# Gate, up and ff1 with tokens stationary, and all moving weights read as two halves of a chunk in turn

## The chip, the cores and the metric

The kernel runs on one core of one Trainium2 chip. The metric is the device time of one execution in microseconds (us), smaller is better. The core's engines are TensorE (PE in the profile, its weight loads PEld), VectorE (DVE), ScalarE (ACT), GpSimd (POOL) and SyncE (SP), which issues nearly all the transfers.

## The reference

Two transformer blocks of width 2048 run one after the other on one sequence of 256 tokens. Cut to what matters here:

```python
def conv_ffn(x, w_gate, w_up, conv_w, conv_b, w_down):        # first block; D_FF = 5632
    hg = x @ w_gate
    hg = causal_conv3_per_channel(hg, conv_w) + conv_b
    return (gelu(hg) * (x @ w_up)) @ w_down

# first block:  h += mix(rmsnorm(h) @ w_in) @ w_out;  h += conv_ffn(rmsnorm(h), ...)
#               h += sigmoid(rmsnorm(h) @ w_ple_gate) * (p @ w_ple_proj)
# second block: mod = silu(c) @ w_mod + b_mod  ->  sh1, sc1, g1, sh2, sc2, g2
#               x += g1 * (attention(h @ w_in_2 ...) @ w_out_2)
#               h = rmsnorm(x) * (1 + sc2) + sh2
#               u = relu(h @ w_ff1)                            # 8192 columns
#               x += g2 * ((u * u) @ w_ff2)
```

All inputs are float32. In total about 510 MB of weights are read once.

## The kernel before

Every dense product is computed in three matmuls of the type float32r. Each operand is split into a high part (a copy rounded to float32r) and a low part (the rest), and high x high, high x low and low x high are accumulated in PSUM.

Weights come in blocks. A block is 256 rows of K by one chunk of 512 output columns (448 or 384 in two chunks), 512 KB, laid out by the host (`_pack`, line 152) so that one transfer fills a tile of 128 partitions x 1024. `prep` (line 273) issues that transfer on SP, has ACT write the high part `whi` (line 281) and DVE the low part `wlo` (line 282). It does so at high priority; there are four buffers of `raw` and three of each part. Some last or first blocks of a stage are kept in tiles of their own (`hold`, names such as `whiaaaaa`). The chunk of K rows that belongs to one matmul is `w[:, j*cw:(j+1)*cw]`, j = 0, 1.

Two forms of product use these blocks:

- `linear` (line 297): 128 tokens are the stationary operand, the weights of one j are the moving operand with `cw` columns (512), and PSUM gets tokens x output columns. A block is 2 token tiles x 2 j x 3 = 12 matmuls (lines 318 to 320). It serves w_in, w_out, w_down, the ple products, w_in2, w_out2, ff2, and the first chunk of ff1.
- `linear_t` (line 346): 128 columns of the weights are the stationary operand and 256 tokens are the moving one, so the result is already transposed (output columns on partitions, tokens along the free dimension), as the convolution over tokens and the next product need it. A block is 4 x 2 x 3 = 24 matmuls of 256 columns (lines 360 to 362). It serves gate and up (11 chunks each) and ff1's chunks 1 to 15. For it, `prep` shifts the weights by 16 elements inside a tile that is 64 elements longer.

Where `linear` is used and a transposed result is wanted, `xt_chunk` (line 385) waits a tick, lets PE transpose four 128x128 pieces into an `aux` bank of PSUM (line 382) and splits the result into high and low parts.

The program is written as a stream of blocks. After each block, `tick` (line 250) moves on the generators that were handed to `spawn`: a generator that yields n goes on n blocks later. `tick` also emits, at a rate `mod_rate` per block, halves of the `w_mod` product (`mod_half`, line 910: a transfer of 512 KB into one of two `wmod` tiles and one multiplication with sum on DVE, line 920). 192 halves are needed, 160 of them before the ple gate; the last 32 run at one per block in ff1. The order of the instructions on each engine is set by a scheduler from priorities and dependencies.

`conv_ffn` (line 963) goes through groups of four chunks (the last has three): gate, then up for each chunk, and the `down` product of a group after the first chunk of the next one. In `conv` (line 981), DVE multiplies the PSUM result by `rb`, the row of 1/rms per token (line 984), ACT applies the first tap and the bias, DVE adds two more taps; after the gelu, DVE multiplies by `rb` again (line 996), for the up product, which `up` (line 1001) takes from PSUM as it is. `mlp2` (line 1402) has the same order with ff1 and ff2 in four groups of four chunks. Its `g2` row comes from the sums of `w_mod`: `mod_row` (line 935) adds up the columns on DVE, transposes them on PE two ticks later (line 940), and writes and reads back a row through DRAM; it is spawned after `ff1(4)`, before the first `ff2`.

Of the kernel before, what the change touches and what calls it, by code (L numbers as in the profile page):

```python
# [9 lines left out]
F32 = mybir.dt.float32  # L10
F32R = mybir.dt.float32r
# [6 lines left out]
P = 128  # L18
# [133 lines left out]
def _pack(w, widths, nk=2):  # L152
    k = w.shape[0]
    out = []
    c0 = 0
    for cw in widths:
        b = w[:, c0:c0 + cw].reshape(k // (nk * P), nk, P, cw).transpose(0, 2, 1, 3)
        out.append(np.ascontiguousarray(b).reshape(-1))
        c0 += cw
    return np.concatenate(out)  # L160


def layout(inputs):
# [25 lines left out]
    a["w_uq"] = _pack(uqc, [CW] * 3, nk=3)  # L189
    ukv = sq("w_ukv_2").reshape(128, 8, 256)  # L190
    a["w_ukv"] = _pack(np.concatenate([ukv[:, :, :128].reshape(128, 1024),
                                       ukv[:, :, 128:].reshape(128, 1024)], axis=1),
                       [2 * CW] * 2, nk=1)
# [11 lines left out]
    return {k: np.ascontiguousarray(v) for k, v in a.items()}  # L205

# [5 lines left out]
class K:  # L212
# [60 lines left out]
    def prep(self, src, ncol, hold=None, shift=False):  # L273
        nc = self.nc
        pool, n, k = (self.HOLD, len(hold), hold) if hold else (self.W, 3, "")
        with self.tc.high_priority():
            raw = self.t(self.W, [P, 1024], "raw", 4)
            self.wdma = nc.sync.dma_start(raw[:, :ncol], src)
            e, s = (0, 0) if hold else (64, 16 * shift)
            hi, lo = (self.t(pool, [P, 1024 + e], w + k, n, F32R)[:, s:s + 1024] for w in ("whi", "wlo"))  # L280
# [16 lines left out]
    def linear(self, xt, name, seq, off, cw, evac, before=None):  # L297
# [9 lines left out]
        def products(c, b, i, w):  # L307
# [6 lines left out]
            for j in range(2):  # L314
                xh, xl = xt(2 * b + j)
                wh = w[0][:, j * cw:(j + 1) * cw]
                wl = w[1][:, j * cw:(j + 1) * cw]
# [27 lines left out]

    def linear_t(self, xt, name, off, evac):


        nc = self.nc
        ps = [self.ps.tile([P, 512], F32, name=self.n("mm"), tag="mm", bufs=4) for _ in range(2)]  # L350
        last = KT // 2 - 1
        for b in range(KT // 2):
            hi, lo = self.prep(self.wblock(name, off + b * 2 * P * CW, 2, CW), 2 * CW, shift=True)
            for m in range(4):
                o = ps[m // 2][:, (m % 2) * T:(m % 2 + 1) * T]
                for j in range(2):
                    xh, xl = xt(2 * b + j)
                    ws = slice(j * CW + m * P, j * CW + (m + 1) * P)
                    first = b == 0 and j == 0 and m % 2 == 0
                    nc.tensor.matmul(o, hi[:, ws], xh, start=first, stop=False, skip_group_check=True)  # L360
                    nc.tensor.matmul(o, hi[:, ws], xl, start=False, stop=False, skip_group_check=True)  # L361
# [1153 lines left out]
```

## Time and profile before

| | us |
|---|---|
| median of 3 runs | 2290.66 |
| lowest and highest | 2286.03, 2298.77 |
| profiled execution, its time | 2293.44 |
| profiled execution, its span (first to last instruction) | 2291.7 |

| engine | busy share of the span | instructions |
|---|---|---|
| PE | 98% | 13714 |
| PEld | 87% | 13714 |
| DVE | 69% | 2329 |
| ACT | 48% | 1560 |

The page of the profile gives busy times per engine, a picture of the span in 40 slices (a digit is tenths busy, for PEclk tenths of the full TensorE clock), and the chain of work that ended last. Views of the trace give single instructions in order of time, groups by line, tables of stretches, and who waited for whom. The durations of matmuls overlap: the next one starts long before the end that is shown, so a rate is read from starts. A name such as `mm<-whi,xt` is the output tile and the operands.

### The profile page before, as it was taken

Reading aid. Unit: us, or ns where it says so; the run is one execution under the profiler, and the core shown is the slowest. Engines: PE = TensorE matmul, PEld = TensorE weight load, DVE = VectorE, ACT = ScalarE, POOL = GpSimd, SP = SyncE. Lnnn points to the kernel's source line nnn. Section 1 sums busy time; section 2 is a strip of 40 time slices with the busy share of each in tenths; the row PEclk is TensorE's granted clock in tenths of the full one; section 3 lists DMA queues with packets and bytes.
Section 4 is the critical chain, followed back from the end, with each engine's and each line's share of the span. In section 5 each row is a group of like instructions: output and inputs, shape, how many; then the busy total and the mean of one; then the engine's idle time right before and its main releaser. Section 6 shows DMA issues by size and latency. Waiting matters only on the chain.

```text
span 2291.7 us, 34932 instructions
## 1 busy us (share of the span) xinstructions
PE 2246.7 (98%) x13714; PEld 1996.9 (87%) x13714; DVE 1573.5 (69%) x2329; ACT 1105.6 (48%) x1560; POOL 25.8 (1%) x35
## 2 busy tenths in 40 slices
PE   9999999999999999999999999999999999999998
PEld 7787887899998999989987788888878998998986
DVE  6777766777876677767777866768766555555555
ACT  6655554454444444434445655655433443443444
POOL 0000000000000000000000000000000000000000
PEclk9999999999999999999999999999999999999999
DMA  8665566677777777777778643566886566656554
GB/s 300 229 211 193 205 230 208 241 254 259 265 264 261 265 252 254 256 258 264 249 255 301 241 161 117 173 194 212 309 290 193 190 187 193 190 187 193 190 188 154
DMA packets 147537, 517.82 MB, mean 226 GB/s; under 512 B 17115, under 2 KB 21292, under 8 KB 146860
## 3 DMA queue, kind: packets, MB, share of 16 engines
q1 hardware_dynamic: 147228, 515.58, 66.3%
q8 instruction: 107, 1.75, 0.3%
q14 instruction: 58, 0.48, 0.1%
q10 hardware_dynamic: 144, 0.01, 0.0%
HBM read 513.38 MB, written 2.14 MB: 225 GB/s over the span
## 4 chain that ended last, share of the span: by engine, by line
PE 80%; DMA 7%; issue 6%; DVE 5%; ACT 1%; POOL 1%; SPq 0%; DVEq 0%; ACTq 0%; POOLq 0%
PE mm L320 14%; PE mm L319 14%; PE mm L318 14%; PE mm L362 11%; PE mm L361 11%; PE mm L360 11%; DMA wmod<-in_w_mod 6%; DVE wlo L282 2%; PE aux L382 1%; DVE wmod L920 1%; PE aux L750 1%; ACT whi L281 1%; DMA raw<-in_w_ff 0%; PE aux L824 0%; PE aux L1273 0%
## 5 line engine op out<-in xcount | busy, mean ns | idle before, releaser
L281 ACT ACTIVATE whi<-raw 128x1024 fp32r<-128x1024 f32 (+1 forms) x746 | 785.9, 1055 | 999.0 <-PE mm L320 539.9
L282 DVE TENSOR_TENSOR wlo<-raw,whi 128x1024 fp32r<-128x1024 f32 (+1 forms) x746 | 905.5, 1216 | 503.6 <-ACT whi L281 501.9
L362 PE MATMUL mm<-xt,wlo 128*128 128x256 f32 x2368 | 662.6, 280 | 5.8 <-DVE wlo L282 5.8
L361 PE MATMUL mm<-xt,whi 128*128 128x256 f32 x2368 | 661.5, 279 | 0.0
L360 PE MATMUL mm<-xt,whi 128*128 128x256 f32 x2368 | 661.5, 279 | 0.0
L361 PEld LDWEIGHTS mm<-xt,whi 128*128 128x128 f32 x2368 | 451.0, 190 | 0.3
L362 PEld LDWEIGHTS mm<-xt,wlo 128*128 128x128 f32 x2368 | 444.6, 188 | 7.4 <-DVE wlo L282 7.2
L360 PEld LDWEIGHTS mm<-xt,whi 128*128 128x128 f32 x2368 | 444.6, 188 | 0.3
L319 PE MATMUL mm<-wlo,hid 128*128 128x512 f32 x848 | 331.4, 391 | 1.0 <-DVE wlo L282 1.0
L318 PE MATMUL mm<-whi,hid 128*128 128x512 f32 x848 | 331.6, 391 | 0.0
L320 PE MATMUL mm<-whi,hid 128*128 128x512 f32 x848 | 331.2, 391 | 0.0
L920 DVE SCALAR_TENSOR_TENSOR wmod<-wmod,cact 128x1024 f32<-128x1024 f32 x192 | 234.5, 1221 | 109.3 <-DMA wmod<-in_w_mod 108.5
L318 PE MATMUL mm<-whi,xt 128*128 128x512 f32 (+2 forms) x660 | 260.3, 395 | 0.9 <-ACT whi L281 0.9
L319 PE MATMUL mm<-wlo,xt 128*128 128x512 f32 (+2 forms) x660 | 256.9, 389 | 3.5 <-DVE wlo L282 3.5
L320 PE MATMUL mm<-whi,xt 128*128 128x512 f32 (+2 forms) x660 | 256.3, 389 | 0.0
L319 PEld LDWEIGHTS mm<-wlo,hid 128*128 128x128 f32 x848 | 159.9, 189 | 35.1 <-DVE wlo L282 2.3
L318 PEld LDWEIGHTS mm<-whi,hid 128*128 128x128 f32 x848 | 159.9, 189 | 33.0
L320 PEld LDWEIGHTS mm<-whi,hid 128*128 128x128 f32 x848 | 159.8, 188 | 33.1
L319 PEld LDWEIGHTS mm<-wlo,xt 128*128 128x128 f32 x660 | 124.5, 189 | 29.3 <-DVE wlo L282 6.6
L318 PEld LDWEIGHTS mm<-whi,xt 128*128 128x128 f32 x660 | 124.3, 188 | 24.6 <-ACT whi L281 1.6
L320 PEld LDWEIGHTS mm<-whi,xt 128*128 128x128 f32 x660 | 124.4, 188 | 23.7
L318 PE MATMUL mm<-whi,mix 128*128 128x512 f32 x244 | 97.9, 403 | 0.0
(349 smaller groups left out, 1796.6 us busy)
## 6 DMA issues: line engine op xcount, KB each, us to landing
raw<-in_w_ff SPq DMA_DIRECT2D x256, 512.0 KB, 3.7
wmod<-in_w_mod SPq DMA_DIRECT2D x192, 512.0 KB, 5.0
raw<-in_w_in SPq DMA_DIRECT2D x120, 512.0 KB, 4.1
raw<-in_w_gate SPq DMA_DIRECT2D x88, 512.0 KB, 3.8
raw<-in_w_up SPq DMA_DIRECT2D x88, 512.0 KB, 4.2
raw<-in_w_down SPq DMA_DIRECT2D x88, 512.0 KB, 4.0
raw<-in_w_out SPq DMA_DIRECT2D x64, 512.0 KB, 3.8
raw<-in_w_pg SPq DMA_DIRECT2D x32, 512.0 KB, 4.6
```

What stands on the lines that cost most here:

```text
L281: nc.scalar.activation(hi[:, :ncol], raw[:, :ncol], AF.Copy)
L282: nc.vector.tensor_tensor(lo[:, :ncol], raw[:, :ncol], hi[:, :ncol].bitcast(F32), op=ALU.subtract)
L318: nc.tensor.matmul(o, xh[:, sl], wh, start=st and j == 0, stop=False)
L319: nc.tensor.matmul(o, xh[:, sl], wl, start=False, stop=False)
L320: nc.tensor.matmul(o, xl[:, sl], wh, start=False, stop=en and j == 1)
L360: nc.tensor.matmul(o, hi[:, ws], xh, start=first, stop=False, skip_group_check=True)
L361: nc.tensor.matmul(o, hi[:, ws], xl, start=False, stop=False, skip_group_check=True)
L362: nc.tensor.matmul(o, lo[:, ws], xh, start=False, stop=(b == last and j == 1), skip_group_check=True)
L382: self.nc.tensor.transpose(pt[:, j * P:(j + 1) * P], src[:, j * P:(j + 1) * P], self.ident)
L750: nc.tensor.transpose(pt[:, jo * P:(jo + 1) * P], L[:, j * P:(j + 1) * P], self.ident)
L920: nc.vector.scalar_tensor_tensor(raw, raw, 1.0, self.cact[:, us], op0=ALU.mult, op1=ALU.mult, accum_out=self.macc[:, j, u:u + 1])
```

## The change

Gate, up and ff1's chunks 1 to 15 use `linear` like all other products; `linear_t` is gone. For gate and up, a new `proj` evicts each token tile on ACT with the scale 1/rms of its tokens, and one tick later lets PE transpose the two tiles back into two `aux` banks, from which the convolution and the up product read; the two multiplications by `rb` and the row `rsb` are gone. ff1 takes the way its first chunk had. The host packs every chunk whose weights are a moving operand with its even columns first and its odd columns behind them, and `moving` gives the matmul an access pattern that takes one column of the first half, one of the second, and so on, so that the output columns are in the old order; `w_uq` and the first part of `w_ukv`, whose weights are partly stationary, keep the plain order there (`turn`). The offset and the longer weight tile in `prep` are gone. The rest of the `w_mod` halves and `mod_row` come before `ff1(4)` instead of behind it, with the transpose five ticks later.

```diff
-def _pack(w, widths, nk=2):
+def _pack(w, widths, nk=2, turn=()):
...
-    for cw in widths:
-        b = w[:, c0:c0 + cw].reshape(k // (nk * P), nk, P, cw).transpose(0, 2, 1, 3)
+    for n, cw in enumerate(widths):
+        b = w[:, c0:c0 + cw]
+        if n not in turn:
+            b = np.concatenate([b[:, 0::2], b[:, 1::2]], axis=1)
+        b = b.reshape(k // (nk * P), nk, P, cw).transpose(0, 2, 1, 3)
...
+def moving(w):
+
+    return w.rearrange("p (a b) -> p b a", a=2)
...
-    def prep(self, src, ncol, hold=None, shift=False):
+    def prep(self, src, ncol, hold=None):
...
-            e, s = (0, 0) if hold else (64, 16 * shift)
-            hi, lo = (self.t(pool, [P, 1024 + e], w + k, n, F32R)[:, s:s + 1024] for w in ("whi", "wlo"))
+            hi, lo = (self.t(pool, [P, 1024], w + k, n, F32R) for w in ("whi", "wlo"))
...
-                wh = w[0][:, j * cw:(j + 1) * cw]
-                wl = w[1][:, j * cw:(j + 1) * cw]
+                wh = moving(w[0][:, j * cw:(j + 1) * cw])
+                wl = moving(w[1][:, j * cw:(j + 1) * cw])
...
-    def linear_t(self, xt, name, off, evac):
...
-    def mod_row(self, rows, k0, tmp):
+    def mod_row(self, rows, k0, tmp, wait):
...
-        yield 2
+        yield wait
...
-            rsb = self.t(F, [P, T], "rsb")
-            self.spread(rsb, rs, F)
-            rb = rsb.unsqueeze(1).to_broadcast([P, 2, T])
+            def proj(name, c, then):
+                tok = [self.t(F, [P, 512], "t2", self.t2b) for _ in range(2)]
+
+                def evac(i, ps):
+                    nc.scalar.activation(tok[i], ps, AF.Copy, scale=rs[:, i:i + 1])
+
+                def post():
+                    yield 1
+                    for jp in range(2):
+                        pt = self.aux().rearrange("p (j t) -> p j t", j=2)
+                        for j in range(2):
+                            for i in range(2):
+                                cj = 2 * jp + j
+                                nc.tensor.transpose(pt[:, j, i * P:(i + 1) * P], tok[i][:, cj * P:(cj + 1) * P], self.ident)
+                        then(jp, pt)
+                self.chunk(xg, name, c * D * CW, KT, CW, evac)
+                self.spawn(post())
...
-                def conv(jp, ps):
-                    js = slice(2 * jp, 2 * jp + 2)
-                    g = self.t(F, [P, 512], "t2", self.t2b).rearrange("p (j t) -> p j t", j=2)
-                    nc.vector.tensor_tensor(g, ps, rb, op=ALU.mult)
+                def conv(jp, pt):
...
-                        nc.scalar.activation(yj, g[:, j, :], AF.Identity, bias=G("conv_b", ch), scale=w[2])
+                        nc.scalar.activation(yj, pt[:, j, :], AF.Identity, bias=G("conv_b", ch), scale=w[2])
...
                     if jp == 1:
                         nc.scalar.activation(y, y, AF.Gelu_apprx_tanh)
-                        for k in range(2):
-                            ks = slice(2 * k, 2 * k + 2)
-                            nc.vector.tensor_tensor(y[:, ks, :], y[:, ks, :], rb, op=ALU.mult)
...
-                self.linear_t(xg, "w_gate", c * D * CW, conv)
-                self.linear_t(xg, "w_up", c * D * CW, up)
+                proj("w_gate", c, conv)
+                proj("w_up", c, up)
...
-                if c == 0:
-                    self.linear(xg, "w_ff1", self.seq_in(2), lambda c_: 0, CW, lambda c_, i, ps: evac(i, ps))
-                else:
-                    self.linear_t(xg, "w_ff1", c * D * CW, evac_t)
+                seq = self.seq_in(2) if c == 0 else [(0, b) for b in range(8)]
+                self.linear(xg, "w_ff1", seq, lambda c_: c * D * CW, CW, lambda c_, i, ps: evac(i, ps))
...
+                    if g == 1 and n == 0:
+                        self.mod_upto(96)
+                        self.spawn(self.mod_row([g2], 80, F, 5))
                     ff1(4 * g + n)
...
-                    if g == 1 and n == 0:
-                        self.mod_upto(96)
-                        self.spawn(self.mod_row([g2], 80, F))
```

Left out: the same use of `moving` in lines 1287 and 1312, the calls of `_pack` for `w_uq` and `w_ukv`, the other two taps, which read `pt` too, and `mod_row`'s first call, which keeps its wait of 2.

## Rows read from the trace of the kernel before

**Rows 1.** The page: busy time by engine; PE's granted clock in 40 slices.
```profile
PE 2246.7 (98%) x13714; PEld 1996.9 (87%) x13714; DVE 1573.5 (69%) x2329; ACT 1105.6 (48%) x1560; POOL 25.8 (1%) x35
...
PEclk9999999999999999999999999999999999999999
```

**Rows 2.** The page: the chain that ended last, shares by line.
```profile
PE mm L320 14%; PE mm L319 14%; PE mm L318 14%; PE mm L362 11%; PE mm L361 11%; PE mm L360 11%; DMA wmod<-in_w_mod 6%; DVE wlo L282 2%; PE aux L382 1%; DVE wmod L920 1%; PE aux L750 1%; ACT whi L281 1%; DMA raw<-in_w_ff 0%; PE aux L824 0%; PE aux L1273 0%
```

**Rows 3.** Stretches (length, PE busy, PEclk, DMA share, GB/s): three of `linear_t`'s seven; sum.
```profile
467.80:688.20 220.40, 219.39 (x1931) 1.00 0.76 261
...
1579.10:1676.50 97.40, 91.58 (x778) 1.00 0.88 307
...
2127.00:2194.90 67.90, 67.90 (x578) 1.00 0.59 186
sum 838.00, PE 831.17; mean PE 118.74
```

**Rows 4.** Line 318, its three large groups (ns, minimum/median/maximum).
```profile
L318 PE MATMUL mm<-whi,hid x848: 387/389/774, 688.3 to 2270.3; 128*128 128x512 f32 x170
...
L318 PE MATMUL mm<-whi,xt x660: 334/389/798, 6.7 to 1578.4; 128*128 128x512 f32 x149, 128*128 128x448 f32 x8, 128*128 128x384 f32 x8
...
L318 PE MATMUL mm<-whi,mix x244: 387/389/628, 367.8 to 1539.7; 128*128 128x512 f32 x122
```

**Rows 5.** Timeline (start, duration, instruction), PE, `linear`: a matmul and the 37th.
```profile
999.78 0.39 PE L318 MATMUL mm<-whi,hid 128*128 128x512 f32 x1
...
1007.94 0.39 PE L318 MATMUL mm<-whi,hid 128*128 128x512 f32 x1
```

**Rows 6.** Timeline, PE, `linear_t` at 500 us: a matmul and the tenth.
```profile
499.90 0.28 PE L360 MATMUL mm<-xt,whi 128*128 128x256 f32 x1
...
500.92 0.28 PE L360 MATMUL mm<-xt,whi 128*128 128x256 f32 x1
```

**Rows 7.** Timeline, PE, `linear` on weights in held tiles: 22 matmuls.
```profile
1292.08 0.39 PE L318 MATMUL mm<-whiaaaaa,xt 128*128 128x512 f32 x1
...
1296.88 0.39 PE L318 MATMUL mm<-whiaaaaa,xt 128*128 128x512 f32 x1
```

**Rows 8.** Transposes (line 382): timeline of four, then their group with its idle time.
```profile
419.16 0.65 PE L382 MATMUL aux<-ident,h 128*128 128x128 f32 x4 [1.12 <-DVE h L891]
...
419.57 0.48 PE L320 MATMUL mm<-whi,mix 128*128 128x512 f32 x1
...
L382 PEld LDWEIGHTS aux<-ident,h 128*128 128x128 f32 x64 | 7.3, 140 | 4.6 <-DVE h L891 2.5 <-DVE h L1016 1.7
```

**Rows 9.** Durations by line: bf16 warm-up, plain fp32, `linear_t`.
```profile
L492 PE MATMUL aux<-junk x12: 379/631/631, 1.2 to 5.4; 128*128 128x512 bf16 x12
...
L781 PE MATMUL aux<-PT,V x24: 377/380/382, 141.9 to 397.7; 128*128 128x256 f32 x24
...
L360 PE MATMUL mm<-xt,whi x2368: 276/281/367, 467.8 to 2194.5; 128*128 128x256 f32 x198
```

**Rows 10.** Stretches, all engines (PE, PEld, DVE, ACT, POOL): the first mixer.
```profile
0.00:468.00 468.00, 452.45 (x2138) 371.27 (x2139) 336.56 (x628) 252.46 (x455) 17.48 (x23) 0.99 0.65 228
```

**Rows 11.** Waits between 1579 and 1712 us (total, times, longest).
```profile
DVE wmod L920 <- DMA wmod<-in_w_mod: 26.8, 22, 2.4
```

**Rows 12.** Groups by line: DVE 460 to 1200 us, ACT 1772 to 2195.
```profile
L984 DVE TENSOR_TENSOR t<-mm,rsb 128x512 f32<-128x512 f32 x22 | 14.6, 684 | 0.0
L996 DVE TENSOR_TENSOR y<-y,rsb 128x512 f32<-128x512 f32 x22 | 14.6, 685 | 1.2 <-ACT y L993 1.1
...
L1424 ACT ACTIVATE t<-mm 128x512 f32<-128x512 f32 x21 | 12.4, 590 | 5.2 <-PE mm L362 5.2
```

**Rows 13.** Timeline, PE, around the transpose of line 940.
```profile
1702.50 0.38 PE L940 MATMUL aux<-ident,modT 128*16 128x128 f32 x1 [3.62 <-DVE modT L932]
...
1703.11 0.63 PE L319 MATMUL mm<-wlo,hid 128*128 128x512 f32 x1
1703.54 0.63 PE L320 MATMUL mm<-whi,hid 128*128 128x512 f32 x1
```

More of the change, by code (lines that the diff above doesn't have):

```diff
@@ L188, in layout @@
                           uq[:, :, 128:].reshape(384, 512)], axis=1)
-    a["w_uq"] = _pack(uqc, [CW] * 3, nk=3)
+    a["w_uq"] = _pack(uqc, [CW] * 3, nk=3, turn=(0, 1))
     ukv = sq("w_ukv_2").reshape(128, 8, 256)
-    a["w_ukv"] = _pack(np.concatenate([ukv[:, :, :128].reshape(128, 1024),
-                                       ukv[:, :, 128:].reshape(128, 1024)], axis=1),
-                       [2 * CW] * 2, nk=1)
+    a["w_ukv"] = np.concatenate([_pack(ukv[:, :, :128].reshape(128, 1024), [2 * CW], nk=1, turn=(0,)),
+                                 _pack(np.concatenate(np.split(ukv[:, :, 128:].reshape(128, 1024), 2, axis=1)),
+                                       [CW])])
     a["w_out2"] = _pack(sq("w_out_2"), [CW] * NCH)
@@ L344, in linear @@
                         self.tick()
-    def linear_t(self, xt, name, off, evac):
[L349 to L361, printed above, removed]
-                    nc.tensor.matmul(o, lo[:, ws], xh, start=False, stop=(b == last and j == 1), skip_group_check=True)
-                if b == last and m % 2 == 1:
-                    evac(m // 2, ps[m // 2].rearrange("p (j t) -> p j t", j=2))
-            self.tick()
     def chunk(self, xt, name, off, nkt, cw, evac, before=None):
@@ L1286, in expand @@
                     for l_, r_ in ((xh, hi), (xh, lo), (xl, hi)):
-                        nc.tensor.matmul(pq, l_, r_, start=(k == 0), stop=(k == 8))
+                        nc.tensor.matmul(pq, l_, moving(r_), start=(k == 0), stop=(k == 8))
                         k += 1
@@ L1311, in expand @@
                     for k, (l_, r_) in enumerate(((ch[:, sl], hi), (ch[:, sl], lo), (cl[:, sl], hi))):
-                        nc.tensor.matmul(pq, l_, r_[:, ws], start=(k == 0), stop=(k == 2))
+                        nc.tensor.matmul(pq, l_, moving(r_[:, ws]), start=(k == 0), stop=(k == 2))
                     nc.scalar.activation(vb[:, i, 4 * n:4 * n + 4, :].rearrange("p h d -> p (h d)"), pq, AF.Copy)
@@ L1372, in out_proj2 @@
         g1 = self.g1
-        self.spawn(self.mod_row(g1, 32, M))
+        self.spawn(self.mod_row(g1, 32, M, 2))
         ss = self.t(self.C, [P, 2, 4], "ss", 2)
@@ L1420, in evac @@
                     self.spawn(self.xt_chunk(r, (hi, lo), i, F))
-                def evac_t(jp, ps):
-                    js = slice(2 * jp, 2 * jp + 2)
-                    r = self.t(F, [P, CW], "t2", self.t2b).rearrange("p (j t) -> p j t", j=2)
-                    nc.scalar.activation(r, ps, AF.Relu)
-                    nc.vector.tensor_tensor(r, ps, r, op=ALU.mult)
-                    self.split(r, hi[:, js, :], lo[:, js, :])
-                if c == 0:
-                    self.linear(xg, "w_ff1", self.seq_in(2), lambda c_: 0, CW, lambda c_, i, ps: evac(i, ps))
-                else:
-                    self.linear_t(xg, "w_ff1", c * D * CW, evac_t)
+                seq = self.seq_in(2) if c == 0 else [(0, b) for b in range(8)]
+                self.linear(xg, "w_ff1", seq, lambda c_: c * D * CW, CW, lambda c_, i, ps: evac(i, ps))
                 hid[c] = (hi, lo)
```

8 lines of the change are left out of this document (4 added, 4 removed).

## Prediction, made before the changed kernel was run

> **What bounds the kernel now.** [...] The first six lines of the chain that ended last, 75% of the span, are the six matmul lines, three of `linear` and three of `linear_t` [rows 2]. So the time is close to a count of matmuls times their spacing, and the next question is what the spacing is. The table of stretches separates the two forms: seven stretches hold all 296 blocks of `linear_t` (11 chunks of gate, 11 of up, 15 of ff1, 8 blocks each) and last 838.0 us together, with PE busy 831 us of it [rows 3]. The forms of one line give the rest: 1752 instructions in the three large groups of line 318 [rows 4], 1840 with its six small groups, and as many on 319 and 320: 5520, in 460 blocks of 12.
>
> [...] In `linear` 36 matmuls of 512 columns take 8.16 us, 226.7 ns each [rows 5]. In `linear_t` 256 columns take 113.3 ns in the first stretch (9 in 1.02 us) [rows 6], and 118 ns in the last one (576 in 67.9 us) [rows 3]. [...] It is also a matter of where the operand lies: the same matmul on weights in a held tile takes 228.6 ns (21 in 4.80 us) [rows 7]. [...]
>
> **The change, part by part.**
>
> *Form of gate, up and ff1.* 296 blocks of 24 matmuls of 256 columns become 296 blocks of 12 of 512: 3552 matmuls, the same number of columns. At the present 226.7 ns they take 805.2 us. What comes back are 8 transposes per chunk, 37 x 8 = 296 instructions (ff1's first chunk has them already). In the trace four of them, from the first one's start to the next product's start, take 419.16 to 419.57, 0.41 us, so 0.10 us each; with the idle time of their weight loads, 4.6 us over 64, it is 0.17 us each [rows 8]. That bounds them at 30 and 51 us; I take 35, nearer the lower end, since the new ones are placed one block (2.7 us) behind an eviction of two 0.6 us activations. 805.2 + 35 - 838.0 = +2 us. At the present spacing the reshaping is therefore worth nothing: everything hangs on the next part.
>
> *Weights read as two halves in turn.* All 5520 + 3552 matmuls with moving weights then take their columns alternately from two places half a chunk apart. No operand of the trace is read like this, so the cost is bounded from rows. Below: a 512-column matmul of bf16 at the end of the warm-up has a duration of 379 ns at least, against 389 (median) for the 512 columns of line 318 [rows 4, 9]: 10 ns go when the moving operand is half as wide, to 216.7 ns. [...] I take 10 ns saved. [...] The price: 5520 x 10 ns = 55 us in `linear`, and 3552 x 10 = 35.5 us in the reshaped part.
>
> [...]
>
> *How much of the gain arrives.* 55 + 35.5 - 2 = 88 us is what PE would save if it were never short of work. It is short in three places: the first mixer (452 of 468 us busy [rows 10], 104 + 32 blocks), the ple gate and second projections (64 blocks), and ff1's first group, where all 16 DMA engines are at 0.88 and 307 GB/s [rows 3] and DVE waits 26.8 us for `wmod` [rows 11] (about 40 blocks). That is 240 blocks x 12 x 10 ns = 29 us; I let a third, 10 us, be eaten by waits that PE's pace hides today. Elsewhere DMA has room: a gate block with its 0.36 of a `w_mod` half is 713 KB, in 2.70 us 264 GB/s, and a down block in 2.60 us 274 GB/s, under the 307 seen.
>
> *Evictions.* Per chunk of gate and up, ACT gains two 512-column evictions of about 0.59 us (44 in all, 26 us; line 1424 has that size), and DVE loses the two multiplications by `rb` of lines 984 and 996 (44 x 0.684 = 30 us) [rows 12]. The convolution reads PSUM instead of SBUF: line 984, with a PSUM operand, and line 996, without one, both take 0.685 us [rows 12], so I charge nothing. ACT is busy half of the time [rows 1]; a new activation can delay a block's `whi`, and three buffers of weights (8 us) cover that. If the cover failed, each chunk would show a wait of up to 1.2 us, 26 us in all. ff1's evictions keep their number. PE's transposes add a wait for ACT, and behind it stand the next block's products; this is in the 35 us above.
>
> *`mod_row` moved ahead of `ff1(4)`.* Eight halves of `w_mod` (192 less 160 less the 24 of three chunks) are now issued together: eight DMAs on SP among the weights, eight multiplications of 1.3 us on DVE, then the transpose of line 940, its copy and the DMAs of the row. Today PE stands 3.6 us before line 940 and then runs at the lower clock level, with starts 0.43 us apart [rows 13]; with a dozen matmuls at that spacing, about 6 us could go. Against it, the eight halves still have to land (8 x 512 KB at 307 GB/s is 13.7 us) while PE holds three blocks of work, 8 us: up to 6 us of waiting, or 10 with a fall of the clock. I take zero, and -6 to +10 for the range.
>
> *The rest* (packing on the host, `w_uq`, `w_ukv`, the padding and the 64-byte offset of the weight tiles) changes no instruction count; their 30 matmuls with moving weights gain 0.3 us.
>
> **Sum.** The profiled execution took 2293.4 us, 1.7 beyond its span and 2.8 above the median. 2293.4 - 88 + 10 = 2215.4; on the median's footing about 2213 us, 3.4% faster.
>
> **The rivals.** [...] *The reading is worth nothing:* the lost cycles belong to the accumulation in PSUM, which the warm-up lacks (each of its matmuls starts a sum anew), or to the format, and not to the order of reading. Then 2 us remain: 2292 us, 2287 to 2308 by the bounds of the transposes. Against it: 228.6 against 226.7 ns for the same instruction in another place. [...]
>
> **How the numbers follow.** Forecast (213 to 219 ns) 0.58, half 0.10, nothing 0.12, cost 0.20. The range takes in the first three: from 2180 (spacing at the array's 213.3 ns gives 9072 x 3.4 ns = 31 us more than forecast) to 2305 (nothing gained and the transposes near their upper bound). Within 0.5% (11 us, about what a measurement of this kernel can tell from no change) falls most of the third case: 0.09; faster 0.69, slower 0.22.
>
> **What would show it.** Starts of line 318's matmuls 216 to 217 ns apart in the down stretches, which nothing else in the change touches: that one number decides between all four cases. Gate and up blocks of 2.7 us with 0.9 us of transposes per chunk and no PE wait on ACT in front of them. DVE less busy by 30 us. PE's share of the span falling a little in the first mixer. No wait at line 940 with a clock drop behind it. The prediction is wrong if the down stretches keep 87 us (mechanism), or if they shorten to 83 us and the end does not follow (the cover).

## The result, and the profile after the change

The kernel after takes 2257.4 us (median of 4 runs, 2255.7 to 2259.5), against 2290.4 us for the kernel before, measured beside it: a ratio of 0.985, with a 95% interval of 0.982 to 0.988. That is 33 us or 1.5% faster, inside the range of the prediction, but less than half of the 77 us forecast. The profiled span is 2254.3 us, where before it was 2291.7.

First the page of the kernel after: busy time, TensorE's granted clock by slice, the chain by line, and the group of the multiplications by `w_mod` (count | busy, mean ns | idle time before them, and what ended it).

```profile
PE 2167.8 (96%) x10456; PEld 1870.1 (83%) x10456; DVE 1539.5 (68%) x2282; ACT 1128.9 (50%) x1603; POOL 25.9 (1%) x35
...
PEclk9999999999999999999999999999999999999999
...
DMA wmod<-in_w_mod 25%; PE mm L328 14%; PE mm L329 14%; PE mm L327 14%; DVE wlo L291 9%; DVE wmod L908 2%; SPq L288 1%; ACT whi L290 1%; PE aux L370 1%; PE aux L738 1%; DMA raw<-in_w_in 0%; DMA raw<-in_w_ff 0%; PE aux L1269 0%; PE aux L812 0%; POOL qr L397 0%
...
L908 DVE SCALAR_TENSOR_TENSOR wmod<-wmod,cact 128x1024 f32<-128x1024 f32 x192 | 235.0, 1224 | 260.0 <-DMA wmod<-in_w_mod 259.4
```

PE's busy time fell by 79 us [rows 1], but its share of the span went from 98% to 96%: the kernel is less bound by TensorE than it was, at the same granted clock, 0.993 on average in both. The chain says by what. The transfers of `w_mod` stood for 6% of it before [rows 2] and stand for 25% now, with 9% for the `wlo` subtraction behind them, and VectorE (DVE) is idle 259 us ahead of its 192 multiplications by `w_mod`. In the waits of the kernel before (total us, times, longest) the same multiplications had 109 us:

```profile
DVE wmod L920 <- DMA wmod<-in_w_mod: 108.5, 87, 4.5
```

The spacing of matmuls, from the timeline of the kernel after in a down stretch (start, duration, instruction), a matmul and the 37th:

```profile
950.04 0.38 PE L327 MATMUL mm<-whi,hid 128*128 128x512 f32 x1
...
957.81 0.38 PE L327 MATMUL mm<-whi,hid 128*128 128x512 f32 x1
```

36 matmuls in 7.77 us are 215.8 ns each, where the plain order had 226.7 [rows 5]. So reading in turn does what was forecast of it, 10.8 ns for the 10 ns forecast; on all 9072 matmuls that would be 98 us. The stretches (length, then busy time of PE, PEld, DVE, ACT and POOL, PEclk, DMA share, GB/s) say where it arrives: the first down stretch, the second ff2, the first gate and up, ff1's first group, the first mixer.

```profile
680.80:765.00 84.20, 84.03 (x393) 73.19 (x392) 55.18 (x63) 35.44 (x35) 0.00 (x0) 1.00 0.77 271
1842.20:1926.20 84.00, 83.92 (x393) 73.20 (x392) 48.50 (x49) 35.29 (x35) 0.00 (x0) 1.00 0.60 200
454.00:680.80 226.80, 218.61 (x1042) 188.96 (x1041) 159.05 (x207) 119.13 (x140) 0.70 (x1) 1.00 0.72 251
1539.50:1660.00 120.50, 111.05 (x528) 94.71 (x529) 95.16 (x130) 60.62 (x77) 0.56 (x1) 1.00 0.78 269
6.80:454.00 447.20, 428.68 (x2125) 368.15 (x2126) 331.05 (x616) 249.14 (x451) 17.38 (x19) 0.99 0.69 234
```

Behind 1756 us, where no `w_mod` half is left to load, PE is busy through the whole stretch (83.9 of 84.0 us in the second ff2) and nearly everything arrives. In the first gate and up stretch, the 80 blocks that stand before the first down, PE is idle for 8.2 us, and the stretch takes 226.8 us where the five chunk pairs took 220.4 before. What happens there shows in one of PE's stalls. SyncE's queue (SPq), then DVE, then PE, in the timeline of the kernel after; the bracket is the idle time before an instruction and what ended it.

```profile
614.50 4.13 SPq L288 DMA_DIRECT2D raw<-in_w_up  x3
618.67 0.43 SPq L907 DMA_DIRECT2D wmod<-in_w_mod  x1
622.27 7.02 SPq L288 DMA_DIRECT2D raw<-in_w_gate  x3
```

```profile
622.68 0.48 DVE L990 SCALAR_TENSOR_TENSOR y<-aux,gains,y 128x254 f32<-128x254 f32 x1
625.43 1.23 DVE L908 SCALAR_TENSOR_TENSOR wmod<-wmod,cact 128x1024 f32<-128x1024 f32 x1 [2.27 <-DMA wmod<-in_w_mod]
626.58 0.08 DVE L908 DVE_READ_ACCUMULATOR wmod<-wmod,cact 128x1 f32 x1
626.58 3.49 DVE L291 TENSOR_TENSOR wlo<-raw,whi 128x1024 fp32r<-128x1024 f32 x3
```

```profile
625.27 0.38 PE L329 MATMUL mm<-whi,xt 128*128 128x512 f32 x1
625.49 0.38 PE L327 MATMUL mm<-whi,xt 128*128 128x512 f32 x1
627.86 0.48 PE L328 MATMUL mm<-wlo,xt 128*128 128x512 f32 x1 [1.99 <-DVE wlo L291]
```

DVE stands 2.27 us at a multiplication whose transfer is still on its way, with three `wlo` subtractions queued behind it; PE runs out of `wlo` and stands 2.37 us from one matmul's start to the next where 0.22 would do. The totals are in the waits of the kernel after (total us, times, longest):

```profile
DVE wmod L908 <- DMA wmod<-in_w_mod: 259.4, 147, 4.4
...
PEld mm L328 <- DVE wlo L291: 46.5, 50, 2.8
...
PE mm L328 <- DVE wlo L291: 26.8, 32, 2.4
...
SPq L288 <- DVE wlo L291: 1449.8, 668, 8.1
```

The last line closes a ring: SyncE stands 1450 of 2254 us at the next weight load, which waits for a `raw` buffer that DVE's `wlo` sets free. A `w_mod` load behind it goes out only then: above, at 618.67 us, where the issue of the weight loads ahead of it ends at 618.63. The ring is not new: in the kernel before SyncE stood there 1491 us.

### The profile page after: what moved, and what is told of

The parts are those of the page before. It is cut to its first block, busy times and chain, and to the rows that moved or that the text cites. A ratio compares the mean times of both kernels' runs of the same rounds, so it can differ in the third digit from the quotient of the medians.

```text
span 2254.3 us, 28447 instructions
## 1 busy us (share of the span) xinstructions
PE 2167.8 (96%) x10456; PEld 1870.1 (83%) x10456; DVE 1539.5 (68%) x2282; ACT 1128.9 (50%) x1603; POOL 25.9 (1%) x35
## 4 chain that ended last, share of the span: by engine, by line
PE 47%; DMA 27%; DVE 14%; issue 7%; ACT 3%; SPq 1%; POOL 1%; DVEq 0%; ACTq 0%; POOLq 0%
DMA wmod<-in_w_mod 25%; PE mm L328 14%; PE mm L329 14%; PE mm L327 14%; DVE wlo L291 9%; DVE wmod L908 2%; SPq L288 1%; ACT whi L290 1%; PE aux L370 1%; PE aux L738 1%; DMA raw<-in_w_in 0%; DMA raw<-in_w_ff 0%; PE aux L1269 0%; PE aux L812 0%; POOL qr L397 0%
## 5 line engine op out<-in xcount | busy, mean ns | idle before, releaser
L328 PE MATMUL mm<-wlo,xt 128*128 128x512 f32 (+2 forms) x1844 | 702.0, 381 | 22.3 <-DVE wlo L291 21.7
L327 PE MATMUL mm<-whi,xt 128*128 128x512 f32 (+2 forms) x1844 | 705.2, 383 | 0.8 <-ACT whi L290 0.8
L329 PE MATMUL mm<-whi,xt 128*128 128x512 f32 (+2 forms) x1844 | 699.5, 379 | 0.0
L328 PEld LDWEIGHTS mm<-wlo,xt 128*128 128x128 f32 x1844 | 349.5, 190 | 81.5 <-DVE wlo L291 35.5
L327 PEld LDWEIGHTS mm<-whi,xt 128*128 128x128 f32 x1844 | 349.3, 189 | 48.5 <-ACT whi L290 2.0
L329 PEld LDWEIGHTS mm<-whi,xt 128*128 128x128 f32 x1844 | 349.3, 189 | 46.4
L327 PE MATMUL mm<-whi,hid 128*128 128x512 f32 x848 | 322.8, 381 | 0.0
L329 PE MATMUL mm<-whi,hid 128*128 128x512 f32 x848 | 322.4, 380 | 0.0
L327 PE MATMUL mm<-whi,mix 128*128 128x512 f32 x244 | 94.7, 390 | 0.0
L328 PE MATMUL mm<-wlo,mix 128*128 128x512 f32 x244 | 93.0, 381 | 1.7 <-DVE wlo L291 1.7
L329 PE MATMUL mm<-whi,mix 128*128 128x512 f32 x244 | 93.2, 382 | 0.0
L328 PEld LDWEIGHTS mm<-wlo,mix 128*128 128x128 f32 x244 | 46.1, 189 | 9.1 <-DVE wlo L291 2.9
L329 PEld LDWEIGHTS mm<-whi,mix 128*128 128x128 f32 x244 | 46.1, 189 | 6.8 <-DVE mix L304 0.3
L327 PEld LDWEIGHTS mm<-whi,mix 128*128 128x128 f32 x244 | 46.1, 189 | 6.2
L390 ACT ACTIVATE junk<-h 128x512 bf16<-128x512 f32 (+1 forms) x50 | 30.5, 609 | 26.9 <-DVE h L1433 11.2
```

What stands on the lines that cost most here:

```text
L327: nc.tensor.matmul(o, xh[:, sl], wh, start=st and j == 0, stop=False)
L328: nc.tensor.matmul(o, xh[:, sl], wl, start=False, stop=False)
L329: nc.tensor.matmul(o, xl[:, sl], wh, start=False, stop=en and j == 1)
L390: self.nc.scalar.activation(j[:, :n], src, AF.Square, accum_out=acc)
```

## The experiments

Each run was measured beside the kernel before, which took 2287.8 to 2294.1 us (medians) on the three chips used; a difference of a few us between runs of different chips says nothing. Lengths of stretches come from one profiled execution of each kernel.

**1. Reading in turn alone.** The kernel before, with the new packing and reading for `linear` only; `linear_t` is kept.

```diff
+                wh = moving(w[0][:, j * cw:(j + 1) * cw])      # in linear
+                wl = moving(w[1][:, j * cw:(j + 1) * cw])
     linear_t(...)                                               # as before, plain order
```

> The kernel before with one part of the change: all matmuls of linear (5520) read their weights as two halves in turn; gate, up and ff1's chunks 1 to 15 stay in linear_t with plain weights, and mod_row stays where it was. All theories expect line 318's spacing at 215.8 ns instead of 226.7. If all of it arrived, 5520 x 10.8 ns = 60 us would go: 2231 us. Theory A (the multiplications of w_mod on DVE wait for their transfer and hold up the low parts of the weights behind them, wherever w_mod runs) expects a part of the 38 us that belong to stretches with w_mod (first mixer 18, down 11, ple 5, ff2's first group 4) to be lost, about a third: 2240 to 2248. Theory C (the loss sits in the new evictions and transposes of gate, up and ff1) expects the whole gain: 2231 to 2234.

Measured: 2235.4 us (2233.5 to 2239.0), ratio 0.977 (0.974 to 0.980). By stretches of the trace, those of `linear` take 43 us less than before. The other 15 us came unforeseen: in most of its stretches `linear_t` ran at 113.3 ns per 256 columns, where before it had been near 118 in all but the first part; nothing in its code or weights had changed. The total lies between what theory A and theory C expected, and because of those 15 us it decides for neither; of the 60 us that `linear` could give, 43 arrived. Half of the change alone is thus faster than the whole.

**2. The form alone.** The kernel after, with plain packing and plain reading.

```diff
-    return w.rearrange("p (a b) -> p b a", a=2)
+    return w
```

> The changed kernel without the reading in turn: plain packing, plain operands, everything else as changed. All expect a spacing of 226.7 ns in all 9072 matmuls and 30.7 us of transposes: 805.2 + 30.7 - 838.0 = -2 us against the kernel before. Theory A (the landing of w_mod) expects little loss at this pace, 2288 to 2296. Theory C (the new evictions are at fault) expects the same loss as in the changed kernel, some 20 us in the gate and up stretches and 10 in ff1's first group: 2305 to 2320.

Measured: 2308.5 us (2306.6 to 2310.1), ratio 1.008 (1.006 to 1.011): the form costs 18 us where the prediction had 2. That is in theory C's range and above theory A's. By stretches, gate and up take 10 us more than before, 7 of which are the first stretch's quicker `linear_t` in the kernel before (220.4 us; at the slower spacing, in run 11, 227.5), and ff1's first group with the first ff2 takes 7 us more. DVE's wait for `w_mod` is 186 us here, so the form, too, raises it above the 109 us of before, without any quicker matmul.

**3. No wait for the landed half.** The kernel after; the transfers of `w_mod` are issued as they were, but the multiplication reads a tile that lies there already. Its sums are therefore not those of `w_mod`; the run is only a measurement.

```diff
-        nc.vector.scalar_tensor_tensor(raw, raw, 1.0, self.cact[:, us], op0=ALU.mult, op1=ALU.mult,
+        nc.vector.scalar_tensor_tensor(self.t(M, [P, 1024], "wjunk", 1, BF16), self.cact[:, 1024:], 1.0, self.cact[:, us], op0=ALU.mult, op1=ALU.mult,
```

> The changed kernel, but the 192 multiplications of line 908 read a tile that is always there instead of the half of w_mod that has landed (the modulation vectors are therefore not the reference's); the transfers are all still issued into their two tiles. Theory A expects PE's waits for wlo to go nearly everywhere: 45 to 55 of the 59 us that are missing come back, 2202 to 2212 us, and gate and up blocks at 2.70 us as in ff1's later groups. Theory B (the transfers themselves are short of bandwidth at the new pace, so that the weights land late) expects no more than 10 us: 2245 to 2257. Theory C expects nothing: 2250 to 2257.

Measured: 2204.9 us (2202.0 to 2205.4), ratio 0.963 (0.961 to 0.965). 52 us go, and the first gate and up stretch falls from 226.8 to 216.3 us with 31 multiplications in it (28 in the kernel after). But the edit does more than take the wait away. With nothing to wait for, the multiplications also move: 129 of the 160 that stood before the ple gate now run in the first mixer, where the kernel after has 47, and none behind the first gate and up stretch. DVE is then crowded in the mixer, busy 418 of 450 us (331 of 447 in the kernel after), in the same view as above:

```profile
6.50:456.30 449.80, 429.49 (x2128) 368.19 (x2128) 418.33 (x788) 249.01 (x453) 26.93 (x19) 0.99 0.69 234
```

So the 52 us are the difference between two plans; run 9, which keeps the multiplications in their stretches, prices the wait better.

**4. No transfer at all.** As 3, without the 192 loads of `w_mod` (100 MB of the 517).

> As the run without the wait for the landing, and the 192 transfers of w_mod are left out too (100 MB of 515; the modulation vectors are not the reference's). Theory A expects nearly the same time as there, 2198 to 2210. Theory B expects the whole loss to come back only here: 2200, and 30 us or more between the two. Theory C: 2250 to 2257.

Measured: 2204.7 us (2202.6 to 2206.2). The loads themselves cost nothing where no multiplication waits for them, so the weights do not come late for want of bandwidth.

**5. The multiplication written one half later.** Each half is multiplied where the next one's load is issued, about three blocks on.

```diff
             nc.sync.dma_start(raw, self.a["w_mod"][j * P:(j + 1) * P, us])
-        nc.vector.scalar_tensor_tensor(raw, raw, 1.0, self.cact[:, us], ...)
+        self.mod_sums()                  # multiplies the half that was loaded last time
+        self.mlate = (raw, us, j, u)
```

> The changed kernel, with the multiplication of each w_mod half emitted one half later than its transfer (in conv_ffn 2.8 blocks, 7.5 us, later; in ff1's first group one block); nothing is left out. Theory A (DVE stands in front of a multiplication whose transfer has not landed, with wlo queued behind it) expects 35 to 50 of the 59 missing us back: 2207 to 2222. Rival D (the two wmod tiles are what limits: with the multiplication later, a tile is held longer, and the next transfer is issued later by as much) expects no gain, 2250 to 2262.

Measured: 2255.4 us (2252.4 to 2263.8), ratio 0.984 (0.980 to 0.989): nothing gained, and the wait is as it was:

```profile
DVE wmod L918 <- DMA wmod<-in_w_mod: 258.3, 149, 4.6
```

The order of DVE's instructions says why. Count for each half how many `wlo` stand ahead of its multiplication, less the number of weight blocks that SyncE issued before its load; gate, up and down stretches, from the starts in the traces:

```
halves by (wlo ahead of the multiplication) - (blocks issued ahead of the load)
                      -3    -2    -1    +1    +2
before                       85     4
after                 15     74
5, written later      15     74
9, tied (below)                          41    51
```

In this run the multiplications stand exactly where the kernel after has them: the planner that sets the order moved them back. The edit did not do what it says, so it does not speak against the theory. This is worth checking before a failed edit is counted.

The table says one more thing. Most multiplications stand two `wlo` ahead, but 15 stand three ahead since the change, and none before. Count PE's stalls in these stretches, as more than 0.6 us from one matmul's start to that of the next, one that reads `wlo`: none before, 1 in run 1 (quicker reading, old positions), 3 in run 2 (the new positions, old spacing), 19 in the kernel after. 12 of the 19, with 15 of their 21 us, stand behind one of those 15 multiplications.

**6. Other orders of reading.** 15 groups of 16 matmuls ahead of the kernel, all on one operand of 512 columns, which differ only in the order in which its columns are read.

```diff
+        turn = lambda n, a: pr[:, :n].rearrange("p (a b) -> p b a", a=a)
+        pats = [(pr, 512)] * 2 + [(turn(512, a), 512) for a in (2, 4, 8, 32, 128, 256)]
+        pats += [(pr.rearrange("p (a b c) -> p b a c", a=2, c=c), 512) for c in (2, 4, 16)]
+        pats += [(pr[:, :256], 256), (turn(256, 2), 256), (pr[:, 0:1].to_broadcast([P, 512]), 512), (pr, 512)]
```

> The changed kernel with 15 runs of 16 matmuls ahead of it, on a tile of constants, one order of reading per run, their results unused (the time means nothing, some 50 us more). All expect 226.7 ns for 512 columns in plain order and 215.8 for two halves in turn. [...] Theory Q (it is the pattern's form that counts, not the place) expects every pattern of two or more levels at 215.8.

Measured, as stretches of that kernel, one group of 16 each, in the order of the list (length, PE busy, PEclk, DMA share, GB/s): plain; in turn from 2, 4, 8, 32, 128 and 256 pieces; from two halves in runs of 2, 4 and 16 columns; then 256 columns, plain and in turn, and one column 512 times. The plain groups at the start and at the end of the 15 are left out.

```profile
9.56:13.19 3.63, 3.63 (x17) 1.00 1.03 407
13.19:16.64 3.45, 3.45 (x17) 1.00 1.03 368
16.64:21.16 4.52, 4.52 (x18) 1.00 0.59 165
21.16:28.94 7.78, 7.78 (x17) 1.00 0.91 371
28.94:35.88 6.94, 6.94 (x17) 1.00 0.66 240
35.88:43.26 7.38, 7.38 (x17) 1.00 0.00 0
43.26:50.50 7.24, 7.24 (x18) 1.00 0.00 0
50.50:55.85 5.35, 5.35 (x18) 1.00 0.00 0
55.85:59.85 4.00, 4.00 (x17) 1.00 0.00 0
59.85:63.70 3.85, 3.85 (x17) 1.00 0.00 0
63.70:65.61 1.91, 1.91 (x18) 1.00 0.00 0
65.61:67.39 1.78, 1.78 (x18) 1.00 0.04 9
67.39:70.89 3.50, 3.50 (x18) 1.00 0.00 0
```

A sixteenth of each length is the time of one matmul: 226.7 ns plain, 215.8 from two halves, but 282, 486, 434, 461 and 452 from more pieces, and 334, 251 and 240 in runs, all at a granted clock of 1.00. Among these orders only the one that the change uses is quicker than the plain one. Theory Q falls: it wanted 215.8 ns for every pattern of two or more levels.

**7. The row back in its place.** The kernel after, with `mod_upto(96)` and `mod_row` behind `ff1(4)` again, where the kernel before has them.

```diff
+                    ff1(4 * g + n)
                     if g == 1 and n == 0:
                         self.mod_upto(96)
-                        self.spawn(self.mod_row([g2], 80, F, 5))
-                    ff1(4 * g + n)
+                        self.spawn(self.mod_row([g2], 80, F, 2))
```

> The changed kernel with the rest of w_mod and mod_row emitted behind ff1(4) again, the transpose two ticks later, as before. If the move is neutral, as I had put it, the time stays at 2257 within 4 us. If the 6.7 us that PE stands before line 928 in the changed kernel come from the move, 3 to 8 us less, 2249 to 2254. If the move helps, 3 to 8 us more.

Measured: 2252.7 us (2251.5 to 2253.5), ratio 0.983 (0.978 to 0.987), 4.7 us less than the kernel after (6 by the two ratios, whose intervals overlap); the first ff2 stretch falls from 95.9 to 92.2 us. So the move cost something like 5 us.

**8. Written later, and spread more evenly.** As 5, with 0.41 halves per block in place of 0.36, so that fewer are left for the stretches behind.

```diff
-                    self.mod_rate = 0.36
+                    self.mod_rate = 0.41
```

> As the run with the multiplications one half later, and with 0.41 instead of 0.36 halves of w_mod per block up to the ple gate, so that the 17 halves that are now left over and issued together there are spread over the blocks before. Theory A expects another 4 to 9 us less than that run, from the ple stretch (98.5 us in the changed kernel, 91.3 without the wait for the landing), 2200 to 2216; theory B (bandwidth) expects the stretches of gate and up to lose what the ple stretch gains, no change.

Measured: 2234.8 us (2229.2 to 2236.4), ratio 0.974 (0.971 to 0.978): 20 us less than 5. The ple stretches fall from 112 to 102 us and the first ff2 from 95.7 to 90.5; gate, up and down, where more halves now run, don't become longer in sum (727 us against 735). The total is still above the 2200 to 2216 us expected, which had counted on the gain that 5 did not bring.

**9. The order forced.** As 5, and the multiplication is tied behind the `wlo` of the newest block on DVE, so that the planner can't move it ahead of that one.

```diff
+            self.wsub = nc.vector.tensor_tensor(lo[:, :ncol], ..., op=ALU.subtract)     # in prep
...
+        with self.tc.issue_after(self.wsub.ins):
             self.nc.vector.scalar_tensor_tensor(raw, raw, 1.0, self.cact[:, us], ...)
```

> The kernel after, each half's multiplication written one half later, as in e5_sum_later, and in addition tied on VectorE behind the wlo subtraction of the newest block, so that it can't stand ahead of it in VectorE's order. Theory A (the loss is VectorE standing at a multiplication whose transfer has not landed, since the order of VectorE's instructions put it there too early): the idle time of VectorE ahead of the w_mod multiplications falls from 258 us to under 60 us and the time to 2206 to 2222 us, close to the 2205 us of e3_no_landing_wait. Rival D (the wait is only moved: the buffer comes free later, so SyncE issues the next w_mod transfer later and stands with the weight loads behind it): the idle time on VectorE falls, but the time stays at 2240 to 2260 us.

Measured: 2215.8 us (2213.9 to 2219.0), ratio 0.966 (0.963 to 0.970): 40 us less than 5, with every instruction of it kept. The waits of this kernel, its first down stretch, its first gate and up, ff1's first group and first mixer (as above), and DVE's timeline around a half that is issued at 593.4 us:

```profile
DVE wmod L919 <- DMA wmod<-in_w_mod: 52.8, 42, 2.9
...
PE mm L328 <- DVE wlo L291: 9.0, 14, 1.4
```

```profile
654.50:738.20 83.70, 83.70 (x393) 73.38 (x392) 57.71 (x65) 35.59 (x35) 0.00 (x0) 1.00 0.85 273
438.30:654.50 216.20, 216.20 (x1042) 189.66 (x1041) 161.21 (x206) 119.74 (x140) 1.07 (x1) 1.00 0.82 267
1496.50:1617.90 121.40, 112.89 (x530) 95.94 (x530) 95.31 (x131) 60.56 (x77) 0.56 (x1) 0.99 0.79 268
6.50:438.30 431.80, 424.12 (x2124) 366.98 (x2125) 330.93 (x615) 249.29 (x451) 17.24 (x19) 1.00 0.73 242
```

```profile
604.82 1.23 DVE L291 TENSOR_TENSOR wlo<-raw,whi 128x1024 fp32r<-128x1024 f32 x1 [1.32 <-ACT whi L290]
605.96 1.22 DVE L919 SCALAR_TENSOR_TENSOR wmod<-wmod,cact 128x1024 f32<-128x1024 f32 x1
607.10 0.08 DVE L919 DVE_READ_ACCUMULATOR wmod<-wmod,cact 128x1 f32 x1
607.46 1.23 DVE L291 TENSOR_TENSOR wlo<-raw,whi 128x1024 fp32r<-128x1024 f32 x1 [0.27 <-ACT whi L290]
```

The multiplication now starts with no idle time before it, PE is busy in all 216.2 us of the gate and up stretch, and down and gate and up take what they take in 3. The rival, that the wait would only move to SyncE, falls: SyncE does wait for `w_mod` buffers (170 us in 144 times, 43 in 24 times in the kernel after), but PE feels nothing of it. Against run 3 it loses in the ple gate (101.2 us against 91.3), ff1's first group (121.4 against 113.5) and the first ff2 (96.9 against 84.0), and gains 18 us in the first mixer (438.3 us against 456.3 from the span's start), where DVE is not crowded. In ff1's first group a half comes with every block, "one half later" is one block later, and all 32 multiplications still stand two `wlo` ahead.

**11 and 12. Two controls: what the wait cost before, and what the form costs without it.** The kernel before, and experiment 2, each with a multiplication that reads a resident tile. In 12 it is the edit of 3; in 11 it is another, which reads and writes `cact` in place:

```diff
-        nc.vector.scalar_tensor_tensor(raw, raw, 1.0, self.cact[:, us], op0=ALU.mult, op1=ALU.mult,
+        nc.vector.scalar_tensor_tensor(self.cact[:, us], self.cact[:, us], 0.0, self.cact[:, us], op0=ALU.mult, op1=ALU.add,
```

> The kernel before, with the w_mod transfers issued as before but the multiplication on VectorE reading a resident tile in place of the landed one (so the mod rows are wrong and no instruction waits for w_mod to land). It says what the landing wait cost already before the change. If it cost little while TensorE was slower (theory A, by 109 us of VectorE idle at these multiplications before against 259 us after): 2265 to 2288 us. If it cost as much as in the kernel after (52 us there, by e3_no_landing_wait), 2235 to 2245 us.

> e2_form_only (new form, weights read in plain order) with the multiplication on VectorE reading a resident tile, as in e3_no_landing_wait. Theory A (the 18 us that the form cost in e2_form_only were mostly VectorE's wait for w_mod): 2290 to 2303 us, and within 10 us of e11_before_no_wait plus what the 31 us of transposes leave. Rival F (the 18 us are TensorE's own, from transposes and evictions): it lies 15 to 25 us above e11_before_no_wait. From the side of e3_no_landing_wait: 2205 us plus 9072 matmuls at 10.83 ns gives 2303 us where nothing hides the slower reading.

Measured: 2267.6 us (2265.6 to 2270.0), ratio 0.989 (0.985 to 0.992), for the kernel before without the wait, and 2278.5 us (2276.1 to 2280.4), ratio 0.994 (0.992 to 0.996), for the form without it. Against the same kernels with the wait, 27 us go before the change, 30 with the form alone, and 52 in the kernel after. As in 3 the multiplications move into the mixer (134 and 129 of 160 there), so these are differences between plans. Run 11's total is in the range of theory A; run 12's is below theory A's and closer to run 11 than rival F's 15 to 25 us, because the 2303 us had counted on the full 98 us of quicker reading, of which only 2278.5 - 2204.9 = 74 us separate 12 from 3. Most of the rest, 16 us, is missing in the crowded first mixer (458.4 us in 12, 456.3 in 3).

The stretches of run 11 say where the wait cost nothing before: the second and third gate and up (180.9 and 90.5 us) and the first two downs (87.1 each) are as long as in the kernel before. Its 27 us come from the first mixer (15) and from ff1's first group with the first ff2 (16); its first gate and up stretch is 7 us longer, at `linear_t`'s slower spacing.

**10. All of it together.** Experiment 9 with 0.41 halves per block (8) and the row back (7).

> e9_sum_behind with 0.41 halves of w_mod per block in place of 0.36 (as in e8_sum_later_rate) and the last mod row back behind ff1(4) (as in e7_mod_row_back). Theory A (what e9_sum_behind still loses against e3_no_landing_wait lies where halves come at one per block or are caught up at once: line pg 101.2 us against 91.3, ff2 first 96.9 against 84.0, ff1 first 121.4 against 113.5): the rate takes about 10 us from pg and the row 4 to 5 us from ff2 first, so 2196 to 2205 us. Rival R (more halves in gate and up and in the first mixer bring VectorE's waits back there): gate, up and down rise above their 2.70 and 2.62 us per block and the time stays at 2208 to 2220 us.

Measured: 2200.2 us (2193.3 to 2203.6), ratio 0.962 (0.959 to 0.964). Of its waits:

```profile
DVE wmod L919 <- DMA wmod<-in_w_mod: 27.5, 21, 2.9
```

None of them is in gate, up and down any more, which stay at 2.70 and 2.62 us per block, so the rival falls; the ple gate goes from 101.2 to 91.6 us, and the first ff2 from 96.9 to 88.9. This version leaves nothing out, is 3.8% faster than the kernel before and 57 us faster than the kernel after, and lies below the 2213 us of the forecast.

## Why the prediction was right about the spacing and wrong about the time

The gain by stretches, as the prediction's numbers give it (10 ns for each matmul, 10 us eaten in the three places short of work, 2 us for the form shared by chunks) and as the profiled executions have it (us, against the kernel before; from the first matmul of a stretch to that of the next):

```
stretches (matmuls with moving weights)     forecast   after   run 3   run 9
first mixer, ple and second projections,
    ff1's first group (2880)                   18.8     15.2    27.1    27.3
gate and up (2112)                             19.9     -5.0    18.1    18.2
down (1056)                                    10.6      2.0     9.7     9.6
first ff2 (384)                                 3.8     -0.4    11.5    -1.4
all others (2592)                              25.1     25.5    25.2    24.4
sum                                            78.2     37.3    91.5    78.1
```

Run numbers are those of the experiments above. That the sum of run 9 is the forecast's is chance: its first row is 8 us above, its first ff2 5 us below.

*The spacing* was right, in the step and in the size: 215.8 ns where 216 to 217 were to show. The time measured, 2257 us, is near the 2253 that half of the saving and half of its loss give in the same sum, but that is chance: half of the saving would have shown as nearly 222 ns. The forecast rested on rows (bf16 against fp32 [rows 9], held tiles against streamed ones [rows 7]), and that part held; why two halves are the one good order is open: the other orders of run 6, at 240 to 486 ns, do not say. No run shows the 213.3 ns from which the range has its lower end of 2180 us, nor the 213 at which the band of the forecast begins; the quickest that 512 columns ran was 215.8 ns (kernel after and run 6).

*That reading in turn costs*, with 0.20 in the prediction, has its place after all, only elsewhere. Successive columns 16 bytes apart take 461 ns, and 452 when they are 8 bytes apart (run 6): twice the 226.7 ns of the plain order. Two halves in turn, with half a chunk from one column to the next, run at 215.8 ns.

*The form* cost somewhat more than the 2 us forecast: in gate, up, down and the ff stretches, run 12 lies 5 us above run 11, in which `linear_t` ran at its slower spacing throughout. The kernel before had the quicker one in its first part; from there it is 12. Eight transposes per chunk take 0.83 us, 0.10 each: the lower bound of [rows 8]. In the first mixer, which the form's edits do not touch, run 12 lies another 5 us above run 11; both crowd DVE there, with different edits, and that was not pursued. The evictions went as forecast, DVE 34 us less busy and ACT 23 us more [rows 1].

*`mod_row`* was taken at zero and cost about 5 us (run 7). Its wait did not shrink but grew, from 3.6 us [rows 13] to 6.3, as PE's timeline in the kernel after shows:

```profile
1681.95 0.38 PE L329 MATMUL mm<-whi,hid 128*128 128x512 f32 x1
1688.64 0.37 PE L928 MATMUL aux<-ident,modT 128*16 128x128 f32 x1 [6.32 <-DVE modT L920]
```

The granted clock behind it is 0.50 in both kernels: from 1689 to 1693 us here, from 1702.5 to 1706 before.

*The step that failed* is "How much of the gain arrives", and in it "Elsewhere DMA has room", by which gate, up and down were charged no loss. 31 us of gain were forecast there and 3 us of loss came: 34 of the 41 us that are missing. Run 9 gets 28 us there by moving the multiplications behind a `wlo` and leaves nothing out. The three places named as short of work were about right in sum, 15 us where 19 were forecast, but much of what they lost was the same wait and not want of work: run 9 gains 29.5 us in the first mixer alone. The sentence on DMA is true and was the wrong question. Runs 3 and 4 show that the bytes cost nothing; what fails is the order in which DVE stands at them. The evidence stood in the rows in front of me: the transfers of `w_mod` were 6% of the chain [rows 2], and I priced their wait only for ff1's first group [rows 11], not for the gate, up and down stretches. The prediction had named the sign, down stretches of 83 us with an end that does not follow, and the cover of three weight buffers as what would then have failed; but it had asked this cover only about the evictions.

Why the wait cost gate, up and down nothing before and some 31 us after (749.7 us against 718.9 in run 9) takes both parts of the change, as the stalls counted under 5 show: the quicker reading alone (run 1, whose second gate and up stretch passes without one at 2.72 us per block) and the form alone (run 2) bring few. That the 15 multiplications three `wlo` ahead are the larger part is read from the traces; no run moves them alone. An estimate from the page of the kernel after (mean time of a `whi` 1.05 us, of a `wlo` and of a multiplication 1.22; a `w_mod` load lands in 5.4 us, the median) goes the same way. Let PE end block k-3 at 0, and a block take T. `whi` of block k is written by 1.05 us and its `wlo` by 2.27; that sets free the buffer for which SyncE stands, it issues the load of block k+4 and then `w_mod` (0.4 us), which lands 5.4 us later, at 8.1. A multiplication three `wlo` ahead stands before the `wlo` of block k+2; it ends at 9.3, and that `wlo` at 10.5. PE wants it at 4T: 11.3 us at the old 2.83 us per block, 10.8 at 2.70, 10.5 at 2.62. The cover was 0.8 us at the old pace and is used up at the new one; any transfer later than the median then shows as a stall of PE. A multiplication two ahead stands before the `wlo` of block k+3, which PE wants a block later, and by the same working 2.6 us or more are left; the seven stalls behind such ones came with DVE waits of 2.0 to 4.4 us.

## What to carry to other kernels

When the engine that bounds a kernel is made quicker, price every wait that its pace hides today, at the new pace: first the ones that the chain already shows with a few per cent, even if the resource behind them has room. A control that leaves a wait out can move the instruction, too: count where it runs before the difference is called the price of the wait. An instruction that waits for a late transfer costs what is queued behind it on its engine (here three `wlo` behind a wait of 2.27 us, and PE idle for 1.99); put it where the transfer has surely landed, and check in the trace that the order really changed, since a planner can undo an edit. And before copying a way of reading an operand, measure exactly that one: its neighbours here take up to twice the time of the plain order and more (486 ns against 226.7 in run 6).

## What the runs showed of the hardware

- A moving operand of 512 fp32 columns took 226.7 ns in plain order and 215.8 ns read from two halves in turn, but 282 to 486 ns from 4 to 256 pieces, and 240 to 334 ns in runs of 16 to 2 columns from two halves (run 6). One column 512 times took 218.7 ns, still 2.9 more than the two halves.
- 256 plain columns had two spacings in `linear_t`, whose code was the same, 113.3 ns and near 118 ns, over whole stretches. The profiled execution of run 1 was in the quicker one more often than that of the kernel before, which gave 15 us that no edit explains. A difference of that size between two kernels with such matmuls can be this alone.
- 100 MB of transfers less, of 517, changed nothing where no instruction waited for them: 2204.9 us with them, 2204.7 without (runs 3 and 4).
